# Low weight parts of the first feed-forward block, larger token group: an adding transfer instead of a subtraction on VectorE

## The chip, the cores and the metric

The kernel runs on one core of one Trainium2 chip. The metric is the device time of one execution in microseconds (us). Engines are named as the profile names them: PE is TensorE (the matrix unit; PEld is its weight load), DVE is VectorE, ACT is ScalarE, POOL is GpSimd, SP is SyncE, which here only issues transfers.

## The reference, cut to what matters

A two-layer streaming encoder step over 640 tokens (512 prompt, 128 sample), model width 1024: a convolution module, then band attention, each followed by a SwiGLU feed-forward block of hidden width 2816. The change concerns the first of these feed-forward blocks:

```python
def swiglu_ffn(h, g, w_in, w_out):
    a, b = jnp.split(rms_norm(h, g) @ w_in, 2, axis=-1)
    return h + (jax.nn.silu(a) * b) @ w_out
```

All inputs are float32.

## The kernel before, in words

**Split matrix products.** Each float32 operand is split into a high part (rounded to the format `fp32r` that PE multiplies) and a low part, the remainder. A product is three matmuls per 128x128 weight tile, added up in PSUM by `mm3`: high weight times high activation (L170), low weight times high activation (L171), high weight times low activation (L172). `wsplit` brings a piece of a weight matrix from HBM to the tile `raw` with one transfer issued by SP (L139, or L134 for the second matrix), makes `whi` from it on ACT (L150) and `wlo` = `raw` - `whi` on DVE, or partly on POOL (L154). The tiles `raw`, `whi` and `wlo` come from the pool `wp`, which has two buffers of each, so that the tiles of one piece take the place of the tiles of the piece two before it.

**Groups and pairs.** The 640 tokens are worked on in two groups of 256 and 384 (`GR`). In the feed-forward block the 22 hidden slices of 128 are taken in chunks. For each hidden slice `ffn_in` loads one *pair*: the 8 weight tiles of the `a` half and the 8 of the `b` half, 128 x 2048 numbers, 1 MB. It multiplies them with all 8 slices of the input (48 matmuls for one group), then makes `silu(a) * b` and splits it into `hid`. After the pairs of a chunk `ffn_out` brings the second matrix (for a chunk of six slices in four pieces of 128 x 1536, 768 KB each) and adds the products to the residual `h` (L303). Group 0 does 18 slices, then both groups do four slices together (`FC`), and then the larger group, 384 tokens, does the 18 slices in three chunks of six (`FD`): six pairs, four pieces of the second matrix, three times. This last stage is the one that the change touches. In it `wsplit` is called with `pool=0`: the low part is made by DVE alone.

**What sets the order.** A scheduler orders the instructions of each engine by a model of their times; `tc.high_priority(offset=HP)` moves the splits ahead. Every engine then runs its list strictly in that order, and waits on semaphores for the others. No transfer of the kernel before is issued by POOL. `dynamic_dma_scratch_size` sets how many bytes at the start of each SBUF partition are kept for descriptors of transfers that POOL issues; all tiles lie behind them.

Of the kernel before, what the change touches and what calls it, by code (L numbers as in the profile page):

```python
# [10 lines left out]
AF = mybir.ActivationFunctionType  # L11
ALU = mybir.AluOpType
# [30 lines left out]
FD = ((0, 6), (6, 6), (12, 6))  # L43
# [2 lines left out]
NPL = 3  # L46
WE = "vpvp"
CM = 6
HP = 2000
LATE = (0, 1)  # L50
CUT, LCUT = 8, 7
# [26 lines left out]
def tile_trunk(ctx, tc, xT, vecs, hist, w_pw1, w_pw2, w_in0, w_out0, w_in1, w_out1,  # L78
               w_kq, w_v, w_o, rel, kc, vc, y_out, convp_out, convs_out, k_out, v_out):
    nc = tc.nc  # L80
# [11 lines left out]
    def nm(s):  # L92
        uid[0] += 1
        return f"{s}_{uid[0]}"
# [30 lines left out]
    def col(base, i):  # L125
        return vec[:, base + i:base + i + 1]

    def wsplit(src, k, n, parts=1, pool=0, cuts=1, gains=None):
        raw = wp.tile([P, 2048], F32, tag="raw", name=nm("raw"))
        hi = wp.tile([P, 2048], F32R, tag="whi", name=nm("whi"))  # L130
        lo = wp.tile([P, 2048], F32R, tag="wlo", name=nm("wlo"))
        sz = k * n
        if parts > 1:
            nc.sync.dma_start(raw[:, :sz].rearrange("p (m c) -> p m c", m=parts), src)  # L134
        else:
            src = src if len(src.shape) == 2 else src.rearrange("p m c -> p (m c)")
            for i in range(cuts):
                a, b = sz * i // cuts, sz * (i + 1) // cuts
                nc.sync.dma_start(raw[:, a:b], src[:, a:b])  # L139
        if gains is not None:  # L140
            for a, b, gain in gains:
                nc.scalar.activation(out=hi[:, a:b], in_=raw[:, a:b], func=AF.Copy, scale=gain)
                nc.vector.scalar_tensor_tensor(out=lo[:, a:b], in0=raw[:, a:b], scalar=gain,
                                               in1=hi[:, a:b].bitcast(F32), op0=ALU.mult,
                                               op1=ALU.subtract)
            return hi, lo
        with tc.high_priority(offset=HP):
            for i in range(cuts):
                a, b = sz * i // cuts, sz * (i + 1) // cuts
                nc.scalar.activation(out=hi[:, a:b], in_=raw[:, a:b], func=AF.Copy)  # L150
                c = b - (b - a) * pool // 4
                for eng, a, b in ((nc.vector, a, c), (nc.gpsimd, c, b)):
                    if a < b:
                        eng.tensor_tensor(out=lo[:, a:b], in0=raw[:, a:b],  # L154
                                          in1=hi[:, a:b].bitcast(F32), op=ALU.subtract)
        return hi, lo
# [76 lines left out]
    def hp(g, k):  # L233
        g0, n = GR[g]
        return h[:, k, g0:g0 + n]

    def rms(g, gain, engs=SQ, cut=CUT, eng=nc.gpsimd):
        n = GR[g][1]
        bc, _ = rstd_bc([hp(g, k) for k in range(KT)], n, engs, cut, None, eng)
        xh, xl = new_xs(g)  # L240
        for k in range(KT):
            t = tp.tile([P, 384], F32, tag="n1", name=nm("n1"), bufs=NB1)
            nc.vector.scalar_tensor_tensor(out=t[:, :n], in0=hp(g, k), scalar=col(gain, k),
                                           in1=bc, op0=ALU.mult, op1=ALU.mult)
            xsplit(t[:, :n], xh[:, k, :], xl[:, k, :])
        return xh, xl, None, None
# [21 lines left out]
    def xk(x, ks):  # L268
        return [(x[0][:, k, :], x[1][:, k, :]) for k in ks]

    def ffn_in(wsrc, j, xs, hid, jj, groups, pool):
        wh, wl = wsplit(wsrc[j], 16, P, pool=pool)
        for g in groups:
            n = GR[g][1]
            ps = []
            for ab in range(2):
                pt = mmt()
                mm3(pt[:, :n], [(wh[:, (ab * 8 + k) * P:(ab * 8 + k + 1) * P],
                                 wl[:, (ab * 8 + k) * P:(ab * 8 + k + 1) * P]) for k in range(KT)],
                    xk(xs[g], range(KT)))  # L280
                ps.append(pt[:, :n])
            bc = xs[g][2]
            with tc.high_priority(offset=HP):
                s = tp.tile([P, 384], F32, tag="t1", name=nm("t1"))
                t = tp.tile([P, 384], F32, tag="t2", name=nm("t2"))
                if bc is None:
                    nc.scalar.activation(out=s[:, :n], in_=ps[0], func=AF.Silu)
                    nc.vector.tensor_tensor(out=t[:, :n], in0=s[:, :n], in1=ps[1], op=ALU.mult)
                else:
                    nc.vector.tensor_tensor(out=s[:, :n], in0=ps[0], in1=bc, op=ALU.mult)  # L290
                    nc.scalar.activation(out=s[:, :n], in_=s[:, :n], func=AF.Silu)
                    nc.vector.tensor_tensor(out=t[:, :n], in0=ps[1], in1=bc, op=ALU.mult)
                    nc.vector.tensor_tensor(out=t[:, :n], in0=s[:, :n], in1=t[:, :n], op=ALU.mult)
                xsplit(t[:, :n], hid[g][0][:, jj, :], hid[g][1][:, jj, :])

    def out_tile(wts, ch, b, m, g, hid):
        wh, wl = wts
        n = GR[g][1]
        pt = mmt()
        mm3(pt[:, :n], [(wh[:, (b + k) * P:(b + k + 1) * P], wl[:, (b + k) * P:(b + k + 1) * P])  # L300
                        for k in range(ch)], xk(hid[g], range(ch)))
        with tc.high_priority(offset=HP):
            nc.vector.tensor_tensor(out=hp(g, m), in0=pt[:, :n], in1=hp(g, m), op=ALU.add)  # L303

    def ffn_out(wsrc, j0, ch, hid, groups, pool):
        mg = 4 if ch <= 4 else 2 if ch <= 8 else 1
        ws = []
        for m0 in range(0, KT, mg):
            src = wsrc[m0:m0 + mg, :, j0 * P:(j0 + ch) * P].rearrange("m p c -> p m c")
            ws.append(wsplit(src, ch * mg, P, parts=mg, pool=pool))  # L310
            if mg == 4:
                continue
            for m in range(m0, m0 + mg):
                for g in groups:
                    out_tile(ws[-1], ch, (m - m0) * ch, m, g, hid)
        if mg == 4:
            for g in groups:
                for m in range(KT):
                    out_tile(ws[m // mg], ch, (m % mg) * ch, m, g, hid)

    def ffn(pool, w_in, w_out, xs, groups, chunks, pl=0, og=None, cm=CM, pad=(0, 0)):
        for j0, ch in chunks:
            hid = {}
            for g in groups:
                n = GR[g][1]
                t = pool[g].tile([P, pad[g] + 2 * cm * n], F32, tag=f"hid{g}", name=nm("hid"))
                t = t[:, pad[g]:].bitcast(F32R).rearrange("p (s k n) -> p s k n", s=2, k=cm)
                hid[g] = t[:, 0], t[:, 1]
            for jj in range(ch):
                ffn_in(w_in, j0 + jj, xs, hid, jj, groups, pl)  # L330
            ffn_out(w_out, j0, ch, hid, og or groups, pl)
# [24 lines left out]
    for b in range(2, 4):  # L356
        nc.gpsimd.tensor_tensor(out=i4, in0=i4, in1=ident[:, 32 * b:32 * b + 32], op=ALU.add)
    y0 = hp0.tile([P, 2 * CM * 256], F32, tag="hid0", name="y0")
    y = [y0[:, 0:KT * 256].rearrange("p (k n) -> p k n", k=KT),
         cp.tile([P, KT, 384], F32, name="y1", tag="y")]  # L360

    w00 = wsplit(w_pw1[0], 16, P, cuts=4, pool=PL1[0][0])
    with tc.high_priority(offset=2 * HP):
        xs = [rms(0, V_NCONV, SSQ, SCUT, nc.vector), None]
# [4 lines left out]
    def glu(c, g, wh, wl):  # L369
        n = GR[g][1]  # L370
        ps = []
        for ab in range(2):
# [4 lines left out]
            ps.append(pt[:, :n])  # L377
        with tc.high_priority(offset=HP):
            t = tp.tile([P, 384], F32, tag="t1", name=nm("t1"))
# [175 lines left out]
    xs0, xs1 = late[0], late[1]  # L555
    cv.close()
    hid1 = ExitStack()
    hp1 = hid1.enter_context(tc.tile_pool(name="hp1", bufs=1))
    ffn({0: hp0}, w_in0, w_out0, {0: xs0}, (0,), chunks, PFB)
    if FC:  # L560
        ffn({0: hp0, 1: hp1}, w_in0, w_out0, {0: xs0, 1: xs1}, (0, 1), FC)
    ffn({1: hp1}, w_in0, w_out0, {1: xs1}, (1,), FD)
    hid1.close()
    hid0.close()

# [373 lines left out]
    def gate(a, b, hid, jj, c):  # L939
        s, t = tmp("t1"), tmp("t2")  # L940
        add("v", s, a, bca[:, c], ALU.mult)
        nc.scalar.activation(out=s, in_=s, func=AF.Silu)
        add("v", t, b, bca[:, c], ALU.mult)
        add("v", t, s, t, ALU.mult)
        xsplit(t, hid[:, 0, jj, c], hid[:, 1, jj, c])

    def plain(j, jj, q, wts):
# [3 lines left out]
        for ab in range(2):  # L951
# [6 lines left out]
            ps.append(pt[:, :HT])  # L958
        with tc.high_priority(offset=HP):
            gate(ps[0], ps[1], hids[0], jj, c)  # L960
# [124 lines left out]
    for q in range(2):  # L1085
        for k in range(KT):
            x = xg[k // 4][:, k % 4, TH[q]]
            nc.scalar.activation(out=x, in_=h[:, k, TH[q]], func=AF.Copy,
                                 scale=col(V_NFFN + KT, k))
            if k % 2:  # L1090
                hi, lo = raw_slot[k // 4][q]
# [180 lines left out]
```

## Time and profile before

| | |
|---|---|
| median of the runs shown | 1551.69 us (2 runs, 1551.46 to 1551.92) |
| profiled execution, its own time | 1551.3 us |
| its span, first to last instruction | 1549.5 us (1.8 us lie around it) |
| PE busy, share of the span | 1471.7 us, 95% |
| DVE, ACT, POOL busy | 1050.1, 662.4, 443.8 us |
| read from HBM | 187.02 MB |
| mean granted PE clock | 0.984 of full speed |

How to read the rows. In a view of instruction groups a row names line, engine, operation, tiles (written tile first, buffer numbers left out), shapes and count, then after the bar the busy time in us and the mean in ns, and then how long the engine sat idle just before and what ended that. In the timeline a row is start (us from the span's start), duration, engine, line, operation; the bracket is the idle time before it and what ended it. In the view of stretches of time the columns are the stretch, its length, the busy us of PE, PEld, DVE, ACT and POOL with instruction counts, the granted PE clock (1.00 is full), the share of the 16 DMA engines that were busy, and GB/s. In the view of waits a row names who waited for whom, the us in total, the times, and the longest. Matmuls are pipelined, so that a busy PE need not be PE at its peak.

### The profile page before, as it was taken

How to read it: one execution, taken by the hardware profiler on the slowest of the kernel's cores; microseconds unless marked ns; L12 is line 12 of the kernel's file. 1: busy time of each engine (PE TensorE's matmuls, PEld its weight loads, DVE VectorE, ACT ScalarE, POOL GpSimd, SP SyncE). 2: the span in 40 equal slices, each digit the busy share in tenths (PEclk: the TensorE clock that was granted, in tenths of full speed). 3: DMA queues.
4: the chain of work that ended last, by engine and by line, in shares of the span. 5: the costliest groups of instructions: out<-in, count | busy, mean ns of one | idle time of the engine just before them, and what ended most of it. 6: DMA issues, size and time to landing. Idle time of an engine off the chain costs nothing.

```text
span 1549.5 us, 26569 instructions
## 1 busy us (share of the span) xinstructions
PE 1471.7 (95%) x10770; PEld 1398.9 (90%) x10770; DVE 1050.1 (68%) x1863; ACT 662.4 (43%) x1173; POOL 443.8 (29%) x403
## 2 busy tenths in 40 slices
PE   5888998989999999999999999999989999999997
PEld 5878888989999999999988798886989999999997
DVE  6994999988555455457576767566796476476455
ACT  4544454535423323235454445443554244244244
POOL 6865568877501000001321211110411121121110
PEclk9999999999999999999999999998999999999998
DMA  7784434444421333433655545453103213213211
GB/s 236 234 228 142 137 113 159 148 157 153 147 82 55 129 116 129 135 118 126 202 183 201 174 140 205 133 175 114 55 28 109 82 56 109 82 55 109 82 55 68
DMA packets 59658, 199.95 MB, mean 129 GB/s; under 512 B 10128, under 2 KB 22672, under 8 KB 46736
## 3 DMA queue, kind: packets, MB, share of 16 engines
q1 hardware_dynamic: 59248, 197.96, 39.1%
q8 instruction: 84, 1.38, 0.4%
q10 hardware_dynamic: 288, 0.31, 0.1%
q14 instruction: 38, 0.31, 0.1%
HBM read 187.02 MB, written 11.22 MB: 128 GB/s over the span
## 4 chain that ended last, share of the span: by engine, by line
PE 71%; DVE 16%; ACT 3%; issue 3%; DMA 3%; POOL 2%; SPq 0%; POOLq 0%; DVEq 0%; ACTq 0%
PE mm L170 12%; PE mm L172 12%; PE mm L171 12%; PE pb L968 6%; DVE w L437 5%; DVE wlo L154 4%; PE pc L968 4%; PE pa L968 4%; PE pb L170 1%; PE pb L171 1%; PE pb L172 1%; PE pa L172 1%; PE pa L170 1%; PE pc L170 1%; PE pc L172 1%
## 5 line engine op out<-in xcount | busy, mean ns | idle before, releaser
L171 PE MATMUL mm<-x,wlo 128*128 128x256 f32 (+1 forms) x1344 | 416.8, 312 | 15.4 <-DVE wlo L154 14.9
L170 PE MATMUL mm<-x,whi 128*128 128x256 f32 (+1 forms) x1344 | 413.3, 312 | 6.4 <-ACT x L159 3.7
L172 PE MATMUL mm<-x,whi 128*128 128x256 f32 (+1 forms) x1344 | 412.7, 311 | 0.5
L150 ACT ACTIVATE whi<-raw 128x2048 fp32r<-128x2048 f32 (+2 forms) x117 | 197.7, 1694 | 232.6 <-PE mm L172 138.8
L171 PEld LDWEIGHTS mm<-x,wlo 128*128 128x128 f32 x1344 | 257.1, 192 | 18.7 <-DVE wlo L154 17.5
L170 PEld LDWEIGHTS mm<-x,whi 128*128 128x128 f32 x1344 | 254.5, 191 | 11.2 <-ACT x L159 4.1
L172 PEld LDWEIGHTS mm<-x,whi 128*128 128x128 f32 x1344 | 255.1, 191 | 2.9 <-DVE x L160 1.8
L154 DVE TENSOR_TENSOR wlo<-raw,whi 128x2048 fp32r<-128x2048 f32 (+5 forms) x117 | 214.0, 1832 | 62.2 <-ACT whi L150 61.2
L154 POOL TENSOR_TENSOR wlo<-raw,whi 128x1536 fp32r<-128x1536 f32 (+3 forms) x50 | 145.7, 2918 | 69.0 <-ACT whi L150 69.0
L913 POOL TENSOR_TENSOR raw<-raw 128x512 f32<-128x512 f32 x38 | 50.5, 1330 | 332.3 <-DVE raw L913 257.5
L171 PE MATMUL mm<-hid,wlo 128*128 128x256 f32 (+1 forms) x352 | 107.7, 308 | 6.6 <-DVE wlo L154 6.6
L172 PE MATMUL mm<-hid,whi 128*128 128x256 f32 (+1 forms) x352 | 105.8, 307 | 0.2
L170 PE MATMUL mm<-hid,whi 128*128 128x256 f32 (+1 forms) x352 | 104.6, 307 | 0.1
L437 DVE SCALAR_TENSOR_TENSOR w<-gp,dwv,w 128x384 f32<-128x384 f32 x180 | 103.9, 612 | 0.8
L195 POOL TENSOR_TENSOR acc<-sq,sq 128x384 f32<-128x384 f32 (+1 forms) x8 | 8.1, 1006 | 258.2 <-ACT sq L179 258.1
L171 PEld LDWEIGHTS mm<-hid,wlo 128*128 128x128 f32 x352 | 66.0, 188 | 7.8 <-DVE wlo L154 7.8
L417 POOL TENSOR_TENSOR y<-y,cvt 128x256 f32<-128x256 f32 (+1 forms) x60 | 69.3, 1154 | 6.3 <-ACT cvt L416 4.0
L172 PEld LDWEIGHTS mm<-hid,whi 128*128 128x128 f32 x352 | 65.7, 188 | 0.6 <-DVE hid L160 0.6
L159 ACT ACTIVATE whi<-raw 128x1024 fp32r<-128x1024 f32 x38 | 39.4, 1054 | 61.6 <-PE pc L172 18.1
L170 PEld LDWEIGHTS mm<-hid,whi 128*128 128x128 f32 x352 | 65.2, 188 | 0.4 <-ACT hid L159 0.3
L968 PE MATMUL pa<-x0f,whi 128*128 128x320 f32 x228 | 61.2, 316 | 2.5 <-DVE t L913 2.3
L195 POOL TENSOR_TENSOR acc<-acc,sq 128x384 f32<-128x384 f32 (+1 forms) x48 | 52.7, 1097 | 28.9 <-ACT sq L179 27.5
(317 smaller groups left out, 3391.4 us busy)
## 6 DMA issues: line engine op xcount, KB each, us to landing
raw<-in_w_in SPq DMA_DIRECT2D x62, 1024.0 KB
raw<-in_w_out SPq DMA_DIRECT2D x36, 768.0 KB
raw<-in_w_pw SPq DMA_DIRECT2D x22, 1024.0 KB
cache<-in_ck SPq DMA_DIRECT2D x32, 512.0 KB
cache<-in_cv SPq DMA_DIRECT2D x32, 512.0 KB
raw<-in_w_kq SPq DMA_DIRECT2D x8, 1024.0 KB
x<-sc SPq DMA_DIRECT2D x16, 368.0 KB
raw<-in_w_out SPq DMA_DIRECT2D x4, 1024.0 KB
```

Of the source, the lines that this page charges most:

```text
L150: nc.scalar.activation(out=hi[:, a:b], in_=raw[:, a:b], func=AF.Copy)
L154: eng.tensor_tensor(out=lo[:, a:b], in0=raw[:, a:b], in1=hi[:, a:b].bitcast(F32), op=ALU.subtract)
L159: nc.scalar.activation(out=hi, in_=src, func=AF.Copy)
L170: nc.tensor.matmul(ps, wh, xh, start=(i == 0), stop=False)
L171: nc.tensor.matmul(ps, wl, xh, start=False, stop=False)
L172: nc.tensor.matmul(ps, wh, xl, start=False, stop=(i == last))
L195: last["acc"] = eng.tensor_tensor(out=acc[:, :n], in0=prev, in1=s(), op=ALU.add)
L417: nc.gpsimd.tensor_tensor(out=y[g][:, c, :], in0=y[g][:, c, :], in1=pr[:, :n], op=ALU.add)
L437: nc.vector.scalar_tensor_tensor(out=dst, in0=src, scalar=wj, in1=dst, op0=ALU.mult, op1=ALU.add)
L913: ENG[e].tensor_tensor(out=out, in0=a, in1=b, op=op)
L968: nc.tensor.matmul(ps, a[:, c], b[:, k, :], start=(first and k == 0 and i == 0), stop=(k == 3 and i == 2), skip_group_check=not first)
```

## The change

For the 18 pairs of the larger group `wsplit` is called with the new mode `DLO`. ACT makes `whi` as before, and then also writes the tile `wlo` with the negated rounding of `raw`, that is, -`whi`. Then POOL issues a transfer that reads the same 1 MB of weights from HBM a second time and adds it onto `wlo`, so that `wlo` ends as `raw` - `whi`. The subtraction on DVE is gone for these pairs. The pieces of the second matrix keep the old way (`pool = 0`). The space for descriptors grows from 256 to 1024 bytes of each partition, which moves every tile 768 bytes up.

```diff
+DLO = 9
@@ def wsplit(src, k, n, parts=1, pool=0, cuts=1, gains=None):
+        if pool == DLO:
+            with tc.high_priority(offset=HP):
+                nc.scalar.activation(out=hi[:, :sz], in_=raw[:, :sz], func=AF.Copy)
+                nc.scalar.activation(out=lo[:, :sz], in_=raw[:, :sz], func=AF.Copy, scale=-1.0)
+                nc.gpsimd.dma_start(lo[:, :sz], src, accum_op=ALU.add)
+            return hi, lo
@@ def ffn_out(wsrc, j0, ch, hid, groups, pool):
+        pool = 0 if pool == DLO else pool
@@
-    ffn({1: hp1}, w_in0, w_out0, {1: xs1}, (1,), FD)
+    ffn({1: hp1}, w_in0, w_out0, {1: xs1}, (1,), FD, DLO)
@@
-                   dynamic_dma_scratch_size=256)
+                   dynamic_dma_scratch_size=1024)
```

The changed file is eight lines longer; its lines for these steps are L150 (`whi`), L151 (`wlo` = -`raw`), L152 (the adding transfer), L177, L178 and L179 (the three matmuls), L297 to L300 and L166 (`silu(a) * b` and its split), L140 and L135 (SP's loads).

The order of ACT at the third pair of the first chunk. The names end in a running number of the tile: before, the third pair is `whi_5346` from `raw_5345`; `t_633` belongs to the pair two ahead of it, and `hid` from `t_634` is that pair's result. The bracket lists the semaphores waited on: `DMAHW` a transfer issued by SP, `DMASW` one issued by POOL, the others an engine.

```order
L291 ACTIVATE t_633_5273<-t_633_5273 128x384 [waits DVE_49]
L150 ACTIVATE whi_5346<-raw_5345 128x2048 [waits DMAHW5_49,PE_49,Activation_49]
L159 ACTIVATE hid_5216<-t_634_5274 128x384 [waits DVE_49]
L291 ACTIVATE t_640_5337<-t_640_5337 128x384 [waits DVE_49]
L150 ACTIVATE whi_5410<-raw_5409 128x2048 [waits DMAHW6_49,PE_49,Activation_49]
```

The same place of the changed kernel, where the third pair is `wlo_5349` and `whi_5348` from `raw_5347`:

```order
L298 ACTIVATE t_633_5274<-t_633_5274 128x384 [waits DVE_49]
L151 ACTIVATE wlo_5349<-raw_5347 128x2048 [waits DMAHW5_49,DMASW0_49,PE_49]
L150 ACTIVATE whi_5348<-raw_5347 128x2048 [waits PE_49,Activation_49]
L269 ACTIVATE bca<-w_818_6961 128x256 [waits PE_49]
L166 ACTIVATE hid_5216<-t_634_5275 128x384 [waits DVE_49]
L298 ACTIVATE t_640_5339<-t_640_5339 128x384 [waits DVE_49]
```

A second copy of the pair stands on ACT, and it stands ahead of the first: `wlo` is written before `whi`. It waits for PE to be done with the buffer's pair two before, as `whi` did.

POOL in the changed kernel, at the start of the stage (`acc` sums squares for a norm of group 0, `rt` is that norm; before, `rt` followed on `acc` directly and nothing else stood here):

```order
L202 TENSOR_TENSOR acc_6964<-acc_6964,sq_6983 128x256 [waits Activation_49,Pool_49]
L152 DMA wlo_5219<-in_w_in 128x2048 [waits DVE_49,Activation_49]
L237 TENSOR_TENSOR rt_6960<-rst_6988,mhalf 128x2 [waits DVE_49]
L152 DMA wlo_5284<-in_w_in 128x2048 [waits Activation_49]
L152 DMA wlo_5349<-in_w_in 128x2048 [waits DMASW0_49,Activation_49]
```

All 18 adding transfers stand here one after the other, each waiting for ACT's negated copy and, from the third on, for the transfer two before it.

PE where the third pair begins, before (`mm_5351` is the sum of its `a` half, `mm_5312` and `whi_5282` belong to the pair ahead):

```order
L172 MATMUL mm_5312<-x_4424,whi_5282 128x384
L170 MATMUL mm_5351<-x_4424,whi_5346 128x384 [waits DVE_49,Activation_49]
L171 MATMUL mm_5351<-x_4424,wlo_5347 128x384 [waits DVE_49]
L172 MATMUL mm_5351<-x_4424,whi_5346 128x384
L170 MATMUL mm_5351<-x_4424,whi_5346 128x384
```

and in the changed kernel (`mm_5354` is the `a` half, `mm_5379` the `b` half):

```order
L179 MATMUL mm_5314<-x_4424,whi_5283 128x384
L177 MATMUL mm_5354<-x_4424,whi_5348 128x384 [waits DVE_49,Activation_49]
L177 MATMUL mm_5379<-x_4424,whi_5348 128x384 [waits DVE_49]
L178 MATMUL mm_5354<-x_4424,wlo_5349 128x384 [waits DMASW2_49]
L179 MATMUL mm_5354<-x_4424,whi_5348 128x384
```

One matmul of the `b` half has moved ahead, so that two matmuls instead of one stand before the first that needs `wlo`, and that one now waits for the adding transfer in place of DVE.

## The prediction

> **What bounds the kernel now.** I read the view of stretches first, for the stage of the 18 pairs (482 to 725 us) and the stretch ahead of it.
>
> ```profile
> 455.00:482.00 27.00, 27.00 (x190) 27.00 (x189) 10.47 (x16) 7.55 (x11) 0.00 (x0) 1.00 0.23 79
> 482.00:725.00 243.00, 243.00 (x1430) 243.00 (x1430) 126.77 (x153) 78.11 (x90) 9.98 (x11) 1.00 0.36 118
> ```
>
> PE is busy for the whole 243.00 us, at clock 1.00. DVE is busy for 126.77 us, about half. So DVE's work here is no bound, and taking some from it gives PE nothing. The waits of the stage say the same: no row has PE as the one who waits, and the longest rows on ACT and DVE are waits for PE.
>
> ```profile
> engine line waited for: us in total, times, longest us
> ...
> ACT whi L150 <- PE mm L172: 89.8, 27, 6.6
> ...
> DVE wlo L154 <- ACT whi L150: 22.6, 29, 1.4
> ```
>
> The groups of the stage give the sizes of the split, and that the matmuls of the low part had 0.0 us of idle time ahead of them.
>
> ```profile
> L171 PE MATMUL mm<-x,wlo 128*128 128x384 f32 x296 | 99.2, 335 | 0.0
> ...
> L154 DVE TENSOR_TENSOR wlo<-raw,whi 128x2048 fp32r<-128x2048 f32 x19 | 43.6, 2293 | 16.4 <-ACT whi L150 16.4
> L150 ACT ACTIVATE whi<-raw 128x2048 fp32r<-128x2048 f32 x19 | 36.4, 1917 | 66.1 <-PE mm L172 66.1
> ```
>
> Next the timeline of ACT and DVE around one pair, to see how much slack the split has.
>
> ```profile
> 514.85 1.92 ACT L150 ACTIVATE whi<-raw 128x2048 fp32r<-128x2048 f32 x1 [3.09 <-PE mm L172]
> ...
> 523.17 1.92 ACT L150 ACTIVATE whi<-raw 128x2048 fp32r<-128x2048 f32 x1 [2.58 <-PE mm L172]
> ...
> 525.12 2.29 DVE L154 TENSOR_TENSOR wlo<-raw,whi 128x2048 fp32r<-128x2048 f32 x1 [0.78 <-ACT whi L150]
> ```
>
> Each copy starts when PE leaves the buffer, so the distance of two copies, 523.17 - 514.85 = 8.32 us, is PE's time for a pair. PE needs the copied pair one pair later. At 523.17 a buffer comes free, at 527.41 `wlo` is ready (525.12 + 2.29), and PE wants it at 523.17 + 8.32 = 531.49. **The slack is 4.1 us, the whole allowance from free buffer to ready `wlo` 8.3 us.** With two buffers this allowance is fixed.
>
> **What the change removes and adds.** Removed are 18 subtractions of 2.29 us on DVE, 41 us. They lay beside a PE that never waited, so this is worth 0. Added are 18 copies of 1.92 us on ACT, 35 us; ACT was busy for 78.11 of 243 us, and `whi`, now the second copy, is ready 3.9 us after the buffer is free, well inside 8.3. Behind the two copies on ACT stands the split of `hid` of the pair two before, later by 1.9 us; it is needed only by the pieces of the second matrix, and the copies ahead of the last `hid` of a chunk belong to those pieces and are as they were. Also 0. POOL has little else to do here (9.98 us), and the first norm's `rt` stands behind an issue only, not behind a transfer's landing. SP's load of the pair two later waited for DVE's subtraction, which ended 4.2 us after the buffer was free, and now for ACT's second copy, 3.9 us after: no change that counts. The move of all tiles by 768 bytes I take at 0; it has no row, and no reason for a gain or a loss.
>
> What remains is the chain that replaces the subtraction: negated copy, issue on POOL, transfer, PE. The trace has no transfer issued by POOL and none that adds. The nearest is SP's load of the same 1 MB.
>
> ```profile
> 510.75 0.33 SPq L139 DMA_DIRECT2D raw<-in_w_in  x1
> ...
> 511.00:511.50 0.50, 0.50 (x5) 0.50 (x4) 0.20 (x1) 0.27 (x1) 0.00 (x0) 1.00 0.00 0
> 511.50:512.00 0.50, 0.50 (x4) 0.50 (x4) 0.00 (x0) 0.26 (x1) 0.00 (x0) 1.00 1.14 131
> 512.00:513.00 1.00, 1.00 (x7) 1.00 (x7) 0.00 (x0) 0.00 (x0) 0.00 (x0) 1.00 0.53 180
> 513.00:514.00 1.00, 1.00 (x8) 1.00 (x7) 0.00 (x0) 0.00 (x0) 0.00 (x0) 1.00 1.00 426
> 514.00:515.00 1.00, 1.00 (x8) 1.00 (x7) 0.20 (x1) 0.15 (x1) 0.00 (x0) 1.00 0.89 377
> 515.00:516.00 1.00, 1.00 (x8) 1.00 (x7) 0.90 (x2) 1.00 (x1) 0.00 (x0) 1.00 0.00 0
> ```
>
> It is issued at 510.75, its first traffic comes some 1.0 us later, and it is over by 515.0. The DMA share sums to 0.5 x 1.14 + 0.53 + 1.00 + 0.89 = 3.0 us of all 16 engines.
>
> *Engine time of the adding transfer.* Lower bound 3.0 us (the addition costs nothing). It has to read the 1 MB in the tile as well as the 1 MB in HBM, and to write 1 MB; upper bound, if the three passes go one after the other, 9.0 us. I take **6.0 us**, two reads of 3.0 with the write beside them, as the plain load has its write beside its read.
>
> *Issue to first traffic, and the end signal.* For SP the first is 1.0 us. POOL has to write the descriptors with its own cores; I take 1.2 us, with 0.3 us for the signal at the end, an estimate. Lower bound for both 1.0. Upper bound 3.0, from POOL's slowest long instruction in the page:
>
> ```profile
> L154 POOL TENSOR_TENSOR wlo<-raw,whi 128x1536 fp32r<-128x1536 f32 (+3 forms) x50 | 145.7, 2918 | 69.0 <-ACT whi L150 69.0
> ```
>
> *The collision.* SP issues the load of the pair two later when ACT's second copy ends, 3.9 us after the buffer is free. Its traffic begins at about 5.0 and is 3.0 us of engine time, right in the adding transfer.
>
> The sum, from the free buffer: copy to 2.0, first traffic at 3.2, alone to 5.0 (1.8 of 6.0 done, 4.2 left). Then I let both share the engines evenly: the load's 3.0 take until 11.0, the adding transfer has 1.2 left, ends at 12.2, signalled at **12.5 us**. PE comes at 8.3 and has two matmuls that don't need `wlo`, 2 x 0.17: 8.7. It stands still for **3.8 us**.
>
> *How often.* The pair behind it got its buffer 8.3 us later, so it is ready 8.3 + 12.5 = 20.8 us after the first one's free buffer; PE, which was held up, comes to it at about 12.5 + 8.0 = 20.5. No stall to speak of. The third again has its buffer only since the held-up end of the first. So every second pair stalls: three in each chunk of six, 9 in all. The pieces of the second matrix keep their slack. 9 x 3.8 = **34 us**.
>
> *The clock.* A PE that stands still for some us gets half the clock in this trace:
>
> ```profile
> 264.50:267.50 3.00, 0.32 (x4) 0.13 (x3) 3.00 (x5) 0.89 (x1) 3.00 (x2) 1.00 0.03 8
> 268.30:271.60 3.30, 3.30 (x18) 3.30 (x17) 3.30 (x6) 0.73 (x2) 3.02 (x2) 0.50 0.92 308
> ...
> 315.30:317.10 1.80, 0.13 (x2) 0.09 (x1) 1.80 (x3) 1.34 (x1) 1.80 (x2) 1.00 0.00 0
> 317.10:325.00 7.90, 7.90 (x70) 7.90 (x70) 7.76 (x14) 1.34 (x1) 5.66 (x4) 1.00 0.77 259
> ```
>
> After 2.7 us without matmuls (3.00 - 0.32) come 3.3 us at 0.50; after 1.7 us (1.80 - 0.13) the clock stays at 1.00. A stall of 3.8 us is of the first kind, and 3.3 us at half speed lose 1.7 us: 9 x 1.7 = **15 us**. These 1.7 us also cover the 0.3 by which the second pair's transfer would be late.
>
> The Trainium skill, page "TensorE: Matmul & The Clock Gate", Part 1, gives the half clock to an idle window of about 3.4 us; a gap of 2.7 us was enough here, so the row decides, and by the page a stall of under 3.4 us would cost nothing beyond itself.
>
> Sum: 34 + 15 = 49 us on the profiled execution's own 1551.3 us (span 1549.5, 1.8 around it), **1600 us**. The median of the runs shown, 1551.69, lies 0.4 us higher; a measurement tells 2%, 31 us, from no change.
>
> **Rivals.**
>
> *The addition is as cheap as a load* (not slower). Engine time 3.0 us: first traffic at 3.2, 1.8 done at 5.0, 1.2 left and shared until 7.4, signalled at 7.7. That is ahead of PE's 8.7, and nothing changes: 1551 us. With 3.0 us instead of 1.5 for issue and signal it comes at about 9.7, a stall of 1.0 us, too short for the clock: 9 x 1.0, 1560 us. It decides between this and my forecast whether the adding transfer needs less than about 4 us of engine time. For it speaks that the row of the plain load shows the engines idle for half of each pair (share 0.36 in the stage); against it, that the tile must be read too.
>
> The Trainium skill, "DMA: Bandwidth & Descriptors", section "Anatomy of one DMA — SWDGE (gpsimd) path", fits 2.0 us + bytes / 436 GB/s for a transfer from POOL, as an estimate 4.4 us for this 1 MB. By that rule the time is this rival's, 1551 us. No run here shows it, and the page "Collectives: The Full Stack", Stop ④, describes the adding transfer as two reads and one write with the addition free, which would double the bytes read. I leave the rule the chance that I give to this rival.
>
> *The adding transfer is much slower.* At 9.0 us of engine time it has 4.2 left when the load ends at 11.0, and is signalled at 15.5: a stall of 6.8 us. From 11.5 the next pair's adding transfer runs beside it (8.3 + 3.2), which can bring the stall to some 10.5 us. 9 x 6.8 to 9 x 10.5 is 61 to 95, with 15 to 30 for the clock 76 to 125 us: 1627 to 1676 us. The DMA engines alone then need 2 x 9.0 + 2 x 3.0 = 24 us for two pairs against PE's 16.6.
>
> *Faster.* It would take idle time of PE in or right behind the stage, and there is none in the 243 us.
>
> **How the numbers follow.** My forecast 0.45 (with its bounds for issue and signal, and the two transfers of neighbouring pairs overlapping, 1575 to 1630), the cheap addition 0.28 (1550 to 1562), the slow one 0.25 (1627 and up), faster 0.02. The range from 1550 to 1665 leaves out the upper part of the slow case, about a tenth, and the faster one. Slower by over 2% (over 1582.7 us) is the slow case and nearly all of the forecast: 0.66. Within 2%: 0.32.
>
> **What would show it.** In the changed profile: PE idle ahead of L178, released by a transfer into `wlo`, 9 times and about 4 us each, on the first, third and fifth pair of each chunk; a PE clock of 0.5 behind each; DVE about 41 us less and ACT about 35 us more busy without effect; 18.9 MB more read from HBM. Step by step: the traffic of an adding transfer alone on the engines gives its engine time, and the distance from the issue on POOL to its first packet the descriptors' cost. Wrong it would be if the transfer lands within 6.7 us of the negated copy's end, if the load and the adding transfer don't share evenly, or if the stall falls on every pair.

## The result, and the profile after

The changed kernel takes **1597.08 us** (median of 2 runs, 1595.21 to 1598.95) against 1551.69: 1.029 times as long, 95% interval 1.024 to 1.0345, slower by over 2%. 1600 was predicted. The profiled execution took 1598.95 us, its span is 1596.8 us, 47.3 us longer than before. One of the ten executions of the kernel with only its tiles moved ran at a granted clock of 0.75 and took 1813.89 us; its ratio further down leaves it out.

The stretches of the 18 pairs, before and then after, each from the first to the last matmul of a chunk's six pairs (columns as in the prediction):

```profile
506.30:556.30 50.00, 50.00 (x290) 50.00 (x290) 24.62 (x28) 16.29 (x17) 0.00 (x0) 1.00 0.36 118
582.10:632.10 50.00, 50.00 (x290) 50.00 (x290) 24.70 (x28) 16.29 (x17) 0.00 (x0) 1.00 0.37 129
657.00:707.00 50.00, 50.00 (x290) 50.00 (x290) 24.70 (x28) 16.28 (x17) 0.00 (x0) 1.00 0.39 129
```

```profile
508.70:569.80 61.10, 54.17 (x298) 52.94 (x297) 14.10 (x24) 25.55 (x23) 5.09 (x6) 0.97 0.77 197
594.90:658.90 64.00, 54.67 (x290) 53.58 (x290) 13.77 (x23) 25.27 (x22) 4.36 (x5) 0.92 0.76 195
684.00:750.80 66.80, 56.89 (x290) 55.93 (x289) 13.77 (x23) 25.27 (x22) 4.32 (x5) 0.90 0.73 188
sum 191.90, PE 165.73 PEld 162.46 DVE 41.64 ACT 76.09 POOL 13.78; mean PE 55.24 PEld 54.15 DVE 13.88 ACT 25.36 POOL 4.59
```

150.0 us have become 191.9. PE stands idle for 191.9 - 165.7 = 26.2 us of them, and is busy for 15.7 us longer. The clock column explains most of that: 61.1 x 0.03 + 64.0 x 0.08 + 66.8 x 0.10 = 13.6 us. DVE's work fell to about 14 of 61 to 67 us and nothing came of it. The DMA engines' share doubled; the page has 205.90 MB read from HBM, 18.9 more than before, as predicted. The remaining 5 us of the 47.3 lie outside these stretches: 2.4 ahead of them (508.70 against 506.30), where the clock records have two steps of 3.4 us more at half clock than before, and the rest behind them. I did not trace them to an instruction.

The waits of the stage (475 to 775 us) name who PE waits for; before, no row of this view had PE as the one who waits:

```profile
PE mm L178 <- DMA wlo<-in_w_in: 26.2, 10, 5.1
```

On the page, the queue of POOL's transfers, the group of the low part's matmuls, and the time from issue to landing of an adding transfer (last column, us):

```profile
q0 software_dynamic: 2592, 18.88, 6.4%
...
L178 PE MATMUL mm<-x,wlo 128*128 128x256 f32 (+1 forms) x1344 | 424.5, 318 | 41.3 <-DMA wlo<-in_w_in 26.2
...
wlo<-in_w_in POOLq DMA_DIRECT2D x18, 1024.0 KB, 9.3
```

6.4% of 16 engines' span, 0.064 x 1596.8 / 18, is **5.7 us of engine time for one adding transfer**. The timeline around the third pair of the first chunk shows the chain; first ACT, then POOL, then PE:

```profile
521.82 1.92 ACT L151 ACTIVATE wlo<-raw 128x2048 fp32r<-128x2048 f32 x1 [2.77 <-PE mm L178]
...
524.04 0.85 POOL L152 DMA_DIRECT2D wlo<-in_w_in  x1 [12.21 <-ACT wlo L151]
...
530.73 0.51 PE L177 MATMUL mm<-x,whi 128*128 128x384 f32 x2
533.82 0.45 PE L178 MATMUL mm<-x,wlo 128*128 128x384 f32 x1 [2.57 <-DMA wlo<-in_w_in]
```

The buffer is free at 521.82. PE runs out of work that doesn't need `wlo` at 531.25 (533.82 - 2.57), 9.4 us later, and goes on at 533.82, **12.0 us after the free buffer**; 12.5 was predicted. The same reading for all stalls of over 1.2 us between 500 and 760 us, worked out from the starts of ACT's L151 and the gaps of PE:

| chunk, pair | free buffer at | PE is there after | `wlo` lets it go on after | stall |
|---|---|---|---|---|
| 1, first | 500.38 | 9.1 | 11.7 | 2.5 |
| 1, third | 521.82 | 9.4 | 12.0 | 2.6 |
| 1, fifth | 542.07 | 9.1 | 10.6 | 1.5 |
| 2, first | 588.64 | 6.8 | 11.4 | 4.7 |
| 2, third | 610.10 | 8.8 | 11.7 | 2.9 |
| 2, fifth | 631.39 | 9.0 | 10.7 | 1.8 |
| 3, first | 677.72 | 6.8 | 11.9 | 5.1 |
| 3, third | 699.30 | 8.8 | 11.5 | 2.7 |
| 3, fifth | 721.73 | 8.8 | 10.9 | 2.0 |

Nine stalls, on the first, third and fifth pair of each chunk, as predicted; the mean is 2.9 us, 3.8 was predicted. They add up to 25.8 of the 26.2 us of waits; the tenth wait, 0.35 us, is at a sixth pair.

### The profile page after: what moved, and what is told of

It reads as the page before. It is cut to its first block, busy times and chain, and to the rows that moved or that the text cites. A ratio compares the mean times of both kernels' runs of the same rounds, so it can differ in the third digit from the quotient of the medians.

```text
span 1596.8 us, 26614 instructions
## 1 busy us (share of the span) xinstructions
PE 1490.5 (93%) x10770; PEld 1413.9 (89%) x10770; DVE 1006.6 (63%) x1845; ACT 695.4 (44%) x1191; POOL 456.9 (29%) x421
## 3 DMA queue, kind: packets, MB, share of 16 engines
q0 software_dynamic: 2592, 18.88, 6.4%
HBM read 205.90 MB, written 11.22 MB: 136 GB/s over the span
## 4 chain that ended last, share of the span: by engine, by line
PE 60%; DVE 15%; issue 12%; DMA 7%; ACT 3%; POOL 3%; SPq 0%; DVEq 0%; ACTq 0%; POOLq 0%
PE mm L178 9%; PE mm L177 9%; PE mm L179 9%; PE pb L976 6%; DVE w L445 5%; PE pc L976 4%; PE pa L976 4%; DVE wlo L161 3%; DMA wlo<-in_w_in 3%; PE pb L177 1%; PE pb L179 1%; PE pb L178 1%; PE pa L179 1%; PE pa L177 1%; PE pc L177 1%
## 5 line engine op out<-in xcount | busy, mean ns | idle before, releaser
L178 PE MATMUL mm<-x,wlo 128*128 128x256 f32 (+1 forms) x1344 | 424.5, 318 | 41.3 <-DMA wlo<-in_w_in 26.2
L177 PE MATMUL mm<-x,whi 128*128 128x256 f32 (+1 forms) x1344 | 416.3, 316 | 5.9 <-ACT x L166 3.7
L179 PE MATMUL mm<-x,whi 128*128 128x256 f32 (+1 forms) x1344 | 418.3, 315 | 0.9 <-DVE x L167 0.7
L178 PEld LDWEIGHTS mm<-x,wlo 128*128 128x128 f32 x1344 | 261.1, 194 | 48.0 <-DMA wlo<-in_w_in 29.3
L177 PEld LDWEIGHTS mm<-x,whi 128*128 128x128 f32 x1344 | 258.4, 194 | 10.8 <-ACT x L166 4.4
L179 PEld LDWEIGHTS mm<-x,whi 128*128 128x128 f32 x1344 | 259.2, 194 | 3.4 <-DVE x L167 2.3
L157 ACT ACTIVATE whi<-raw 128x2048 fp32r<-128x2048 f32 (+2 forms) x99 | 163.5, 1655 | 170.8 <-PE mm L179 79.1
L161 DVE TENSOR_TENSOR wlo<-raw,whi 128x1536 fp32r<-128x1536 f32 (+5 forms) x99 | 175.0, 1771 | 48.3 <-ACT whi L157 46.7
L178 PE MATMUL mm<-hid,wlo 128*128 128x256 f32 (+1 forms) x352 | 108.1, 309 | 6.8 <-DVE wlo L161 6.8
L179 PE MATMUL mm<-hid,whi 128*128 128x256 f32 (+1 forms) x352 | 106.0, 308 | 0.1
L177 PE MATMUL mm<-hid,whi 128*128 128x256 f32 (+1 forms) x352 | 104.5, 307 | 0.0
L152 POOL DMA_DIRECT2D wlo<-in_w_in x18 | 15.9, 883 | 215.7 <-ACT wlo L151 200.3
L178 PEld LDWEIGHTS mm<-hid,wlo 128*128 128x128 f32 x352 | 66.1, 188 | 8.2 <-DVE wlo L161 8.2
L425 POOL TENSOR_TENSOR y<-y,cvt 128x256 f32<-128x256 f32 (+1 forms) x60 | 65.8, 1097 | 4.6 <-ACT cvt L424 2.2
L166 ACT ACTIVATE whi<-raw 128x1024 fp32r<-128x1024 f32 x38 | 39.4, 1054 | 62.1 <-PE pc L179 18.4
L179 PEld LDWEIGHTS mm<-hid,whi 128*128 128x128 f32 x352 | 65.8, 188 | 0.5 <-DVE hid L167 0.3
L177 PEld LDWEIGHTS mm<-hid,whi 128*128 128x128 f32 x352 | 65.0, 188 | 0.1
```

The source lines that it names most:

```text
L152: nc.gpsimd.dma_start(lo[:, :sz], src, accum_op=ALU.add)
L161: eng.tensor_tensor(out=lo[:, a:b], in0=raw[:, a:b], in1=hi[:, a:b].bitcast(F32), op=ALU.subtract)
L166: nc.scalar.activation(out=hi, in_=src, func=AF.Copy)
L177: nc.tensor.matmul(ps, wh, xh, start=(i == 0), stop=False)
L178: nc.tensor.matmul(ps, wl, xh, start=False, stop=False)
L179: nc.tensor.matmul(ps, wh, xl, start=False, stop=(i == last))
```

## The experiments

**Theory A**, the prediction's: the loss is a chain (negated copy, issue, adding transfer) that is longer than the allowance which two buffers give, plus the half clock behind the stalls. Against it stood that POOL's issue or the second reading of the weights is the cost in itself, that moving the tiles matters, or that each transfer costs PE something. All differences are to the kernel before on the same chip (1550.34 us for the first four, 1551.58 for the next four, 1550.13 for the last).

### The transfer without the addition

```diff
-                nc.gpsimd.dma_start(lo[:, :sz], src, accum_op=ALU.add)
+                nc.gpsimd.dma_start(lo[:, :sz], src)
```

> POOL's transfer only copies the pair onto wlo instead of adding it; copies, order and buffers as in the change (the low part is then wrong: wlo holds the whole weight). Theory A (the sum of the prediction: the second read of the adding transfer is what makes it late): engine time 3.0 us in place of 5.7, landed about 8.5 us after the free buffer, PE comes at 8.7: no stall inside a chunk, some 2 us at the start of the second and third chunk, 1552 to 1558 us. Theory B (a transfer from POOL is late by itself, by POOL's descriptors and its queue, and the addition is free): 9 stalls as in the change, about 1597 us.

Measured: 1555.37 us, ratio 1.0032 (1.0011 to 1.0053). Its page, and its waits from 475 to 760 us:

```profile
q0 software_dynamic: 2592, 18.88, 3.7%
...
wlo<-in_w_in POOLq DMA_DIRECT2D x18, 1024.0 KB, 5.1
```

```profile
PE mm L178 <- DMA wlo<-in_w_in: 1.3, 2, 0.7
```

ACT's second copy, POOL's issue, the order and the 18.88 MB read again are all there, and PE waits for 1.3 us. So it is the addition: it takes the landing from 5.1 to 9.3 us and the engine time from 0.037 x 1547.8 / 18 = 3.2 us to 5.7. The packet records show where: past the first sixteen packets of a transfer, which take longer in both, a packet of 8 KB takes 0.33 us (median) without the addition and 0.63 us with it. The median time lies 5 us above the kernel before, of which the waits explain 1.3; the rest was not traced.

### The tiles moved, and nothing else

The kernel before with one number changed:

```diff
-                   dynamic_dma_scratch_size=256)
+                   dynamic_dma_scratch_size=1024)
```

> The kernel before with 1024 instead of 256 bytes kept for descriptors, so that all tiles lie 768 bytes higher; nothing else. Theory A: no effect, 1551 to 1553 us. Rival D (the new addresses cost something): part of the 45 us is here, 1556 us or more.

Measured: 1549.83 us, ratio 0.999 (0.9971 to 1.0008). Moving the tiles costs nothing.

### Copy and transfer in two halves

```diff
-                nc.scalar.activation(out=hi[:, :sz], in_=raw[:, :sz], func=AF.Copy)
-                nc.scalar.activation(out=lo[:, :sz], in_=raw[:, :sz], func=AF.Copy, scale=-1.0)
-                nc.gpsimd.dma_start(lo[:, :sz], src, accum_op=ALU.add)
+                for i in range(2):
+                    a, b = sz * i // 2, sz * (i + 1) // 2
+                    nc.scalar.activation(out=lo[:, a:b], in_=raw[:, a:b], func=AF.Copy, scale=-1.0)
+                    nc.gpsimd.dma_start(lo[:, a:b], src[:, a:b], accum_op=ALU.add)
+                nc.scalar.activation(out=hi[:, :sz], in_=raw[:, :sz], func=AF.Copy)
```

> The negated copy and the adding transfer are cut in two, for the a half and the b half of a pair; the same bytes. Theory A (the chain from free buffer to landed wlo is longer than the allowance, while the DMA engines have time enough): the first half lands about 7 us after the free buffer, before PE needs it at 8.7, the second by 12, before PE needs it at 12.8; only the starts of the second and third chunk stall by about 1 us: 1552 to 1560 us. Theory C (the DMA engines' total or POOL's work per transfer is the bound): nothing gained or worse, 1590 to 1605 us.

Measured: 1562.17 us, ratio 1.0092 (1.0058 to 1.0126). The waits from 475 to 760 us:

```profile
PE mm L180 <- DMA wlo<-in_w_in: 8.0, 13, 1.3
```

The chain is shorter by the half copy, and PE needs the second half of the tile only in the second half of the pair. 13 waits, none longer than 1.3 us, and no stretch of half clock in the stage: 34 of the 45 us (45.4 - 11.8) are back with the same bytes and the same addition. That is 2 us above what theory A expected, which had waits at the starts of two chunks only.

### A third buffer for `wlo`

In the pairs every third `wlo` lies in a tile of another pool, which is free in this stage; `raw` and `whi` keep two.

```diff
+        if pool == DLO and third[0] % 3 == 0:
+            lo = hp0.tile([P, 2 * CM * 256], F32, tag="hid0", name=nm("wlo"))
+            lo = lo[:, 0:2048].bitcast(F32R)
+        else:
+            lo = wp.tile([P, 2048], F32R, tag="wlo", name=nm("wlo"))
+        third[0] += pool == DLO
```

> A third buffer for wlo of the 18 pairs, in a tile of the smaller group's hidden slices that is free by then; raw and whi keep two. Theory A: the allowance from free buffer to use grows by a pair, from 8.3 to 16 us, the chain of 12 us fits, no stall and no half clock: 1551 to 1554 us. Theory C (the transfers take too much of the DMA engines, or slow PE by their traffic): most of the loss stays, 1575 to 1597 us.

Measured: 1560.51 us, ratio 1.0069 (1.0048 to 1.009). Its page, and its waits from 475 to 760 us:

```profile
wlo<-in_w_in POOLq DMA_DIRECT2D x18, 1024.0 KB, 9.3
```

```profile
PE mm L185 <- DMA wlo<-in_w_in: 4.4, 5, 2.1
```

The transfer lands as late as in the changed kernel, 9.3 us after its issue, and the waits for it fall from 26.2 to 4.4 us. The length of the transfer by itself accounts for little of the loss; its length against the allowance does for most. Theory A expected no stall and no half clock, and the time is 6 us above its range: five waits are left, the longest 2.1 us, and the clock records have one step of 3.4 us at half clock behind that one.

### The adding transfer for every second pair

```diff
+        pool = 0 if pool == DLO and jj % 2 else pool
```

> Only the first, third and fifth pair of each chunk use the adding transfer, 9 instead of 18; the others are subtracted on DVE as before. Theory A (a pair stalls when its chain is longer than the allowance, and the pair behind it then has time): the same 9 stalls at the same places with half the transfers, 1583 to 1597 us. Theory C (the loss is so much per transfer, by load on POOL or the DMA engines): half the loss, about 1573 us.

Measured: 1592.13 us, ratio 1.0271 (1.0228 to 1.0314). The queue on its page, and the waits from 495 to 765 us:

```profile
q0 software_dynamic: 1296, 9.44, 3.3%
```

```profile
PE mm L178 <- DMA wlo<-in_w_in: 27.0, 9, 4.8
```

Half the transfers, the same nine stalls and the same 27 us. A cost for each transfer would have halved. It also shows that the first, third and fifth pairs are late with no adding transfer between them. That the pairs between are covered by the stall ahead of them is read from the change's own trace, where they wait for 0.35 us in all; adding transfers for these pairs alone were not run.

### Without the colliding load

SP's load of `raw` is left out for 17 of the 18 pairs; the copies read the first pair's `raw`, so the weights of the others are not the right ones.

```diff
-        raw = wp.tile([P, 2048], F32, tag="raw", name=nm("raw"))
+        once = pool == DLO and not fixed
+        if once:
+            fixed.append(hp0.tile([P, 2 * CM * 256], F32, tag="hid0", name=nm("raw")))
+        raw = fixed[0] if pool == DLO else wp.tile([P, 2048], F32, tag="raw", name=nm("raw"))
@@
-            for i in range(cuts):
+            for i in range(cuts if pool != DLO or once else 0):
```

> SP's loads into raw are left out for 17 of the 18 pairs: all copies read the first pair's raw, in a tile of its own; copies, adding transfers and buffers as in the change (high and low parts are then those of mixed pairs). Theory A with the collision as a term: the adding transfer has the engines alone, 2.0 to the issue, 1.6 to first traffic, 5.7, 0.4 for the signal, 9.7 us against 8.7: stalls of 1.1 us, 3.2 at the start of the second and third chunk where PE's last piece is shorter, 1560 to 1570 us. Rival E (the collision costs nothing, the adding transfer is slow by itself): 1590 us or more.

Measured: 1580.27 us, ratio 1.0193 (1.0166 to 1.022), between the two expectations. The queue and the landing on its page, and the waits from 475 to 775 us:

```profile
q0 software_dynamic: 2592, 18.88, 6.7%
...
wlo<-in_w_in POOLq DMA_DIRECT2D x18, 1024.0 KB, 8.1
```

```profile
PE mm L183 <- DMA wlo<-in_w_in: 20.3, 10, 3.7
```

Alone, an adding transfer lands after 8.1 us, and the load beside it adds 1.2. The prediction had 7.5 and 3.0. Of the 26.2 us of waits 20.3 are there without a collision.

### The negated copy second

```diff
-                nc.scalar.activation(out=lo[:, :sz], in_=raw[:, :sz], func=AF.Copy, scale=-1.0)
+                nc.scalar.activation(out=lo[:, :sz], in_=hi[:, :sz].bitcast(F32), func=AF.Copy,
+                                     scale=-1.0)
```

It reads `whi`, so it can no longer stand ahead of it on ACT. This lengthens the chain.

> The negated copy reads whi instead of raw, so it comes second on ACT, behind whi and hid: the adding transfer is issued some 2.4 us later, and SP's load of the pair two later 1.9 us earlier, ahead of it. Theory A: the delay of 2.4 us is paid and the collision saved; 4.4 + 1.6 + 5.7 + 0.4 = 12.1 us after the free buffer against some 11.9 in the change, 1594 to 1604 us. Rival E (no collision term): 9 x 2.4 us more, 1615 us or more.

Measured: 1613.29 us, ratio 1.0412 (1.0378 to 1.0445). Its landing, and the waits from 475 to 775 us:

```profile
wlo<-in_w_in POOLq DMA_DIRECT2D x18, 1024.0 KB, 8.1
```

```profile
PE mm L179 <- DMA wlo<-in_w_in: 34.1, 9, 4.4
PE mm L178 <- ACT whi L150: 3.3, 2, 1.7
```

ACT and POOL at the third pair of the first chunk:

```profile
525.01 1.92 ACT L150 ACTIVATE whi<-raw 128x2048 fp32r<-128x2048 f32 x1 [2.87 <-PE mm L180]
...
529.71 0.85 POOL L153 DMA_DIRECT2D wlo<-in_w_in  x1 [14.76 <-ACT wlo L151]
```

The time lies between the two expectations. The issue comes 4.7 us after the free buffer (529.71 - 525.01) instead of 2.2, but the transfer lands after 8.1 us, like the one without a load, so that 1.2 of the 2.5 us of delay come back. The packet records show why: at this pair the load's packets run from 527.91 to 531.31, and the adding transfer's first packet comes at 531.26, so the load is out of its way. The number of stalls stays nine.

### The same idea where DVE is busier

The halves version for the smaller group's 18 pairs, and the larger group as before:

```diff
+                for i in range(2):
+                    a, b = sz * i // 2, sz * (i + 1) // 2
+                    nc.scalar.activation(out=lo[:, a:b], in_=raw[:, a:b], func=AF.Copy, scale=-1.0)
+                    nc.gpsimd.dma_start(lo[:, a:b], src[:, a:b], accum_op=ALU.add)
@@
-        pool = 0 if pool == DLO else pool
+        pool = PFA if pool == DLO else pool
@@
-            ffn({0: hp0}, w_in0, w_out0, {0: late[0]}, (0,), (chunks.pop(0),), PFA)
+            ffn({0: hp0}, w_in0, w_out0, {0: late[0]}, (0,), (chunks.pop(0),), DLO)
@@
-    ffn({1: hp1}, w_in0, w_out0, {1: xs1}, (1,), FD, DLO)
+    ffn({1: hp1}, w_in0, w_out0, {1: xs1}, (1,), FD)
```

> The adding transfers, cut in halves as in the second experiment, at the 18 pairs of the smaller group instead, where DVE also does the convolution and is busy for all of 180 to 320 us; the larger group's pairs as before. Theory A: PE needs only 48 x 0.114 = 5.5 us for a pair there, so the chain of some 12 us stalls it although DVE and POOL are relieved: 1560 to 1600 us. Rival F (DVE bounds that stretch, so 18 x 0.6 us less DVE work tells): 1540 to 1549 us.

Measured: 1586.3 us, ratio 1.0231 (1.0203 to 1.0259). The same stretch of the kernel before and of this one, and the waits of PE from 175 to 420 us, again before and then here:

```profile
180.00:320.00 140.00, 126.25 (x996) 118.87 (x996) 139.65 (x230) 68.79 (x95) 106.66 (x55) 0.98 0.44 141
```

```profile
180.00:320.00 140.00, 111.42 (x855) 103.73 (x853) 116.17 (x209) 84.94 (x113) 73.29 (x66) 0.95 0.83 208
```

```profile
PE mm L171 <- DVE wlo L154: 19.8, 17, 3.6
```

```profile
PE mm L180 <- DMA wlo<-in_w_in: 45.4, 25, 5.9
PE mm L180 <- DVE wlo L163: 3.6, 4, 1.6
```

Here DVE was full before (139.65 of 140 us) and now has air, yet PE does less (111.42 against 126.25), since the pairs of 256 tokens leave a shorter allowance and the transfer misses it. The relief itself is real: PE's waits for DVE's low part fell from 19.8 to 3.6 us. But 45.4 us of waits for the transfer took their place. Taking work from a full engine is of no use when what replaces it is late for PE. A third buffer in this stretch was not run, so whether the 16 us could be had stays open.

### Halves and third buffer together

Both edits from above in one kernel:

```diff
+        if pool == DLO and third[0] % 3 == 0:
+            lo = hp0.tile([P, 2 * CM * 256], F32, tag="hid0", name=nm("wlo"))
...
+                for i in range(2):
+                    a, b = sz * i // 2, sz * (i + 1) // 2
+                    nc.scalar.activation(out=lo[:, a:b], in_=raw[:, a:b], func=AF.Copy, scale=-1.0)
+                    nc.gpsimd.dma_start(lo[:, a:b], src[:, a:b], accum_op=ALU.add)
```

> Third buffer for wlo and the transfer in two halves at once. Theory A (the loss is the adding chain against the allowance of a buffer, plus the half clock that follows a stall): each of the two edits alone left 4.4 and 8.0 us of waits for the adding transfer; together the allowance (16.6 us for the pairs that have the third buffer in reach) is longer than the chain by several us, the waits for the adding transfer fall under 2 us, no half clock is granted in the stage, and the time is 1550 to 1556. Rival F (the adding traffic or the second copy on ACT costs something of its own, in ACT's order or in contention with the loads, beside the waits): the waits for the adding transfer go and 6 us or more stay, 1557 to 1563.

Measured: 1554.25 us, ratio 1.0028 (1.0011 to 1.0045). The stretches of the three chunks, and the queue, the landing and the waits from 475 to 760 us:

```profile
508.40:558.80 50.40, 50.40 (x292) 50.40 (x291) 13.77 (x23) 23.76 (x25) 7.03 (x8) 1.00 0.84 215
584.80:635.20 50.40, 50.40 (x290) 50.15 (x289) 13.77 (x23) 23.65 (x25) 7.75 (x9) 1.00 0.91 238
660.20:711.80 51.60, 50.92 (x291) 50.21 (x290) 13.86 (x23) 23.65 (x25) 7.83 (x9) 1.00 0.90 235
```

```profile
q0 software_dynamic: 5184, 18.88, 6.6%
...
wlo<-in_w_in POOLq DMA_DIRECT2D x36, 512.0 KB, 8.6
```

```profile
PE mm L187 <- DMA wlo<-in_w_in: 0.7, 2, 0.4
```

All 18 pairs take their low parts from adding transfers, the DMA engines are busy for 84 to 91% of the time, and PE is as full as before at full clock: 152.4 us against 150.0 and 191.9. With the allowance longer than the chain, about nine tenths of the loss are gone (4.1 of 45.4 us are left). It doesn't beat the kernel before, where PE had no idle time in this stage to win. Where the last 4 us (0.28%) are lost was not settled; 2.4 lie in the stretches, with 0.7 of waits for the transfer.

## Why the prediction was right, point by point

**What bounds the stage, and that the freed DVE time is worth 0**: right. DVE's busy time fell by 1050.1 - 1006.6 = 43.5 us (predicted 41) and ACT's rose by 695.4 - 662.4 = 33.0 (predicted 35), and neither shows an effect of more than a few us of its own: the kernels without the addition and with halves and third buffer have both and are 5.0 and 4.1 us slower.

**Engine time of the adding transfer, 6.0 us**: right, 5.7 (5.9 alone). A plain transfer from POOL has 3.2 us, so the addition is a factor of 1.8, and two reads with the write beside them fit that. No row shows the second read itself. The Trainium skill, "Collectives: The Full Stack", Stop ④, describes the adding transfer of a collective as two reads and one write, which fits 5.7 against 3.2.

**Issue to first traffic, 1.2 us, and the landing alone, 7.5 us**: both too small. In the packet records of the trace the first traffic comes about 1.6 us after POOL's issue (1.2 for the transfer without the addition), and the landing alone measured 8.1.

**The collision, 3.0 us**: over-sized; 9.3 - 8.1 = 1.2 us. The prediction named it as a sign of being wrong if the two don't share evenly, and they don't. What failed first is when the load runs:

```profile
525.57 0.33 SPq L140 DMA_DIRECT2D raw<-in_w_in  x1
```

In the packet records this load has its first packet at 529.61, 4.0 us after its issue, where the load in the prediction's rows took 1.0. The first packets of the twelve 1 MB loads beside adding transfers come 7.4 to 8.0 us after the free buffer, not 5.0, and each load ends after the adding transfer, so that only part of its 3.0 us can get in the way. Why a load starts so late there is not shown. The two errors, the landing too short and the collision too long, cancel in part: 10.5 us from issue to landing were predicted, 9.3 measured, and from the free buffer 10.6 to 12.0 us (mean 11.4) instead of 12.5.

**PE is there after 8.7 us**: right within 0.7 inside a chunk. It failed at the first pair of the second and third chunk, 6.8 us, where the stalls are the longest, 4.7 and 5.1. What runs there is not a pair but a piece of the second matrix. The timeline of before already showed it, in ACT's copies across that place:

```profile
576.06 1.92 ACT L150 ACTIVATE whi<-raw 128x2048 fp32r<-128x2048 f32 x1 [4.93 <-PE mm L172]
582.30 1.92 ACT L150 ACTIVATE whi<-raw 128x2048 fp32r<-128x2048 f32 x1 [4.32 <-PE mm L172]
```

582.30 - 576.06 = 6.24 us for the last piece, against 8.32 for a pair: the allowance is 2.1 us shorter there, and I took one allowance for all.

**Every second pair, 9 stalls**: right, and borne out by the run with half of the transfers. **34 us of stalls**: 26.2. `wlo` lets PE go on 11.4 us after the free buffer instead of 12.5, and PE is there after 8.5 us on the mean instead of 8.7, so the mean stall is 2.9 us instead of 3.8. The collision, 1.8 us too long, is the term that made it too large.

**15 us for the clock**: 13.6, but not by the predicted steps. I had one stretch of 3.3 us behind each of nine stalls; the clock records have six stretches, at six of the nine, two of them twice as long (6.8 us). That eight steps of 3.4 us come near nine of 3.3 is luck. Rows of two stretches right behind a stall, of 2.5 us and of 1.8 us:

```profile
512.10:515.50 3.40, 3.40 (x11) 3.40 (x12) 0.00 (x0) 0.32 (x1) 0.00 (x0) 0.51 1.07 212
```

```profile
640.40:642.20 1.80, 0.07 (x1) 0.07 (x1) 0.76 (x2) 1.80 (x2) 0.01 (x1) 1.00 0.88 289
642.20:645.60 3.40, 3.40 (x20) 3.40 (x21) 0.56 (x1) 1.79 (x2) 0.87 (x1) 1.00 0.76 169
```

11 matmuls in 3.4 us at 0.51 against 20 at 1.00. Gaps of 2.0, 2.5, 2.7 and 2.9 us brought the half clock here, as did those of 4.7 and 5.1, those of 1.5 and 1.8 did not, and one of 2.6 did not either. The prediction went by the length of the gap. The clock records show that its place counts too: in this stage the half clock begins and ends only at multiples of 3.41 us from 512.14, and the clock of a step follows what PE did in the step before. The step ahead of 512.14, and the two over which the gap of 2.6 us is spread:

```profile
508.73:512.14 3.41, 0.90 (x8) 0.81 (x6) 0.72 (x2) 3.41 (x2) 1.63 (x2) 1.00 0.94 298
529.21:532.62 3.41, 2.04 (x12) 1.71 (x10) 1.12 (x2) 1.86 (x2) 0.00 (x0) 1.00 0.98 286
532.62:536.04 3.42, 2.23 (x12) 2.23 (x13) 0.56 (x1) 2.26 (x3) 0.88 (x1) 1.00 0.79 187
```

PE is idle for 2.5 us of the first, and half clock follows; it is idle for 1.4 and 1.2 us of the other two, and the clock stays. Of the steps at full clock in this stage, all with 2.0 us or more of idle time were followed by half clock, and none with 1.7 us or less. The Trainium skill, "TensorE: Matmul & The Clock Gate", Part 1, asks for an idle window of about 3.4 us; 2.0 us of a step were enough here, and the measurement decides.

**The rival of a cheap addition** fell: 9.3 us to landing, where under about 6.7 was needed. It would have been right without the addition: 5.1 us. (Its 9.7 us for a slow issue and signal depend on how the 3.0 us are divided: by the sum's own steps 2.7 and 0.3 give 10.7, 1.2 and 1.8 give 9.2.) The estimate by the rule of the Trainium skill, "DMA: Bandwidth & Descriptors", section "Anatomy of one DMA — SWDGE (gpsimd) path", 4.4 us, is 0.7 below the plain transfer and half of the adding one. **The slow rival** (9.0 us of engine time) fell too, by the queue's row.

**The sum.** 49 us were forecast, and the span grew by 47.3. But the stage has only 41.9 of these, 7 less than forecast; the total came so close because of 5 us outside the stage, which the sum had at nothing. The mechanism is borne out, the closeness of the number is in part luck.

## What to carry to other kernels

Before work is taken from an engine, look whether anyone waits for it; then compare the new chain, from the free buffer to the ready tile, with the allowance that the number of buffers gives, and do so at each kind of place, since the shortest stretch of work decides, not the usual one. A transfer that is longer than the step it replaces costs little once the allowance covers it: cut in halves and given a third buffer, the same adding transfers went from 2.9% slower to 0.3%. Stalls cost PE more than their length: in this stage 26.2 us of them brought 13.6 us of lost clock.

## What the runs showed of the hardware

- An adding transfer of 1 MB from HBM onto SBUF takes 5.7 to 5.9 us of all 16 engines and lands after 8.1 us alone, 9.3 beside a load; a plain one issued by POOL takes 3.2 us and lands after 5.1. Issuing it takes 0.9 us of POOL's time, 0.55 without the addition.
- Of the 8.1 us alone, about 1.6 pass before the first packet, 6.1 until the last packet ends, and 0.4 until the landing. The first 16 packets take 1.3 us each (median), 0.9 in the plain transfer from POOL; the other 112 take 0.63 us against 0.33, and there lies most of the difference.
- A load beside it delayed the adding transfer by 1.2 us, though the load itself is 3.0 us of engine time. The load was held up more: its first packet came 4.0 us after its issue instead of 1.0.
- In this stage PE's clock changed only at steps of 3.41 us, and fell to half after a step in which PE was idle for 2.0 us or more.
